# Hymba layer on one core: the first output projection's scalings spread over its last norm steps, five of eight transposes within the last query product

## The chip, the core and the metric

One core of a Trainium2 chip. The metric is the device time of one execution in microseconds, as a median over runs. The engines are TensorE (PE in the profile, its weight loads PEld), VectorE (DVE), ScalarE (ACT), GpSimd (POOL) and the DMA queues, which are issued by SyncE (SP) and POOL.

## What is computed

One decoder layer, cut to what matters here; rmsnorm divides a row by its root mean square and multiplies it by a gain.

```python
def layer(x, attend, ..., w_in, w_out, w_up, w_down):
    proj = rmsnorm(x, g_mix_pre) @ w_in
    q, k, v, xl, gate = jnp.split(proj, ...)
    attn = attend(q, k, v)              # stick-breaking attention
    lru = rglru_branch(xl, ...)         # recurrent branch
    mixed = jnp.concatenate([attn, lru * gelu(gate)], axis=-1) @ w_out
    x = x + rmsnorm(mixed, g_mix_post)
    u = jax.nn.relu(rmsnorm(x, g_mlp_pre) @ w_up)
    x = x + rmsnorm((u * u) @ w_down, g_mlp_post)
```

The prompt has 2048 rows and 16 meta tokens, the model 1024 columns, the MLP 4096; 64 sample rows run along. All is float32.

## The kernel before

**Products.** Every float32 operand is split into a high part and a residue (ahi and alo, whi and wlo, uh and ul), and a product is three matmuls per chunk of 128 of the 1024 inner columns: high x high, residue x high, high x residue. In `gemm` they are L184 to L186, with 8 chunks k to one output tile of 128x512; `work.tick` at L190 stands behind chunks 2, 5 and 7. In `gemm_nat` (L194) they are L216 to L218; it serves the output and the down projections. Weights come by DMA into wraw (two buffers); ACT copies them to whi (L161), DVE subtracts to get wlo (L162), two buffers each, one tile ahead.

**Blocks.** The 2048 prompt rows are four blocks s of 512. `inproj` (L434) runs for each s: recurrent branch, keys, values, then `queries` (L588), a generator that yields after each of four query products. At the last block the generator is held back: its products c = 0 and 1 run ahead of the first block's output projection, c = 2 and 3 (the last) behind it.

**Attention** runs on the side. `attn` is a generator of small steps, each with up to three things: logits (L706, into T), then sigmoids, a scan (L650), a carry copy (L653) and a product (L654) on ACT and DVE; the transposing of finished weights beta (L716, into T), which ACT and DVE split into wth (L727) and wtl (L728); and the product with the values (L738, L740, into O). `Work` deals the steps out: `tick(c)` earns c times a rate of engine time and takes steps until it is spent, `burst(us)` takes steps worth that many microseconds at once, `need` takes steps until the named block's attention is finished. PE runs in the order in which the program is written; the order of the other engines' instructions is set by the framework's scheduler.

**The first output projection.** `Group.out_proj` (L987) multiplies the mixed rows of the first block by w_out, in four row blocks j, whose results are y0 to y3 (128x1024 each). `follow(n)` does the norms behind it: `added` (L1003) adds x to the normed y, stores x1 (L1005) and lets ACT sum its squares; `rstd_of` (L236 or L238 on DVE, L240 on POOL) makes the factor by a power. Two `follow` calls and four scalings `normed(j)` (L1010) are left to the caller as a list `todo`: entries 0 and 1 are `follow(3)` and `follow(4)`, entries 2 to 5 scale y0 to y3. `xpose(k)` transposes column block k of all four y (L264, four 128x128 transposes into T); ACT scales that into ahi (L266) and DVE makes alo (L267), both in the tiles that the up products read. Eight such groups come ahead of the first up product.

Ahead of the change the order is: output projection, `todo[0]`, query product 2, `todo[1]`, query product 3, the four scalings, a burst of 4.0, and eight times `xpose(k)` with a burst of 0.5. Then up (`up`, eight products of 128x512) and down (`down`) alternate, four times for each block. The other blocks' output projections stand before the last down products of the block ahead, with a `need` for their attention in front (`group`, L1172), and their norms within those down products.

Of the kernel before, what the change touches and what calls it, by code (L numbers as in the profile page):

```python
# [18 lines left out]
KC = 8  # L19
# [63 lines left out]
def program(tc, I, O, NSB, NSC):  # L83
    with tc.manual_schedule(engines={ET.PE}):
        _program(tc, I, O, NSB, NSC)


def _program(tc, I, O, NSB, NSC):
# [3 lines left out]
    work = Work()  # L92
# [24 lines left out]
    def psD():  # L117
        return T(ps, [P, 512], F32, "D", 4)

    def psT():  # L120
        return T(ps, [P, 512], F32, "T", 3)
# [43 lines left out]
    def w_next():  # L165
        n = wpos[0]
        wpos[0] += 1
        w_split(n)
        w_load(n + 1)
        w_split(n + 1)  # L170
        w_load(n + 2)
        return wsp.pop(n)

    def gemm(ahi, alo, chunks, after_k=None, before_k=None):

        whi, wlo = (t.rearrange("p (k m) -> p k m", k=KC) for t in w_next())
        outs = []
        for ci, (a, b) in enumerate(chunks):
            acc = psD()
            o = acc[:, 0:b - a]  # L180
            for k in range(KC):
                if before_k is not None:
                    before_k(ci, k)
                nc.tensor.matmul(o, whi[:, k, :], ahi(k, a, b), start=(k == 0), stop=False)  # L184
                nc.tensor.matmul(o, whi[:, k, :], alo(k, a, b), start=False, stop=False)  # L185
                nc.tensor.matmul(o, wlo[:, k, :], ahi(k, a, b), start=False, stop=(k == KC - 1))  # L186
                if after_k is not None and ci == len(chunks) - 1:
                    after_k(k)
                if k in (2, 5, 7):
                    work.tick(0.64 * (b - a) / SB * (3 if k < 7 else 2))  # L190
            outs.append(o)
        return outs
# [67 lines left out]
    def xpose_k(ys, k, gT, hi, lo):  # L260

        t = psT()
        for j, y in enumerate(ys):
            nc.tensor.transpose(t[:, j * P:(j + 1) * P], y[:, k * P:(k + 1) * P], ident)  # L264
        n = len(ys) * P
        nc.scalar.activation(hi[:, 0:n], t[:, 0:n], AF.Identity, scale=gT[:, k:k + 1])  # L266
        nc.vector.scalar_tensor_tensor(lo[:, 0:n], t[:, 0:n], gT[:, k:k + 1], hi[:, 0:n].bitcast(F32),  # L267
                                       op0=ALU.mult, op1=ALU.subtract)
# [154 lines left out]
    def prep(s):  # L423

        ys = []
        for j in range(4):
            y = T(xp_, [P, DM], F32, "y", 4)
            nc.sync.dma_start(y, xsrc(s, j))
            r = rstd_of([mean_sq(y, P)], P)
            nc.vector.tensor_scalar(y, y, r, None, op0=ALU.mult)  # L430
            ys.append(y)
        return ys

    def inproj(s, p1, pa, K, ahi, alo, before_k=None):  # L434
# [8 lines left out]
        def stage(nm, d, bufs=2):  # L443
            return T(p1 if nm == "sf" else pa, [P, W], d, nm, bufs)
# [143 lines left out]
        def queries():  # L588
            ys = None
            for c in range(4):  # L590
                nxt = None
                if c == 2 and s + 1 < NSB:
                    ys = prep(s + 1)
                if c == 3 and s + 1 < NSB:
                    def nxt(k):
                        if k > 0:
                            xpose_k(ys, k - 1, K["g_pre"], ahi[:, k - 1], alo[:, k - 1])
                outs = gemm(hi_, lo_, chunks, after_k=nxt)
                if nxt is not None:
                    nxt(KC)  # L600
                hi, lo = stage("sh", F32R), stage("sl", F32R)
                for (a, b), o in zip(chunks, outs):
                    nc.scalar.copy(hi[:, a:b], o)
                    nc.vector.tensor_tensor(lo[:, a:b], o, hi[:, a:b].bitcast(F32), op=ALU.subtract)
                for e, t in ((0, hi), (1, lo)):
                    nc.sync.dma_start(qd[s][2 * c:2 * c + 2, :, e, :].rearrange("h p n -> (h p) n"), t[:, o0:o0 + SB].bitcast(F32))
                if s == 0:
                    a0 = NP - chunks[1][0]
                    for hh in range(2):
                        src = outs[1][64 * hh:64 * hh + 64, a0:a0 + NSAMP].rearrange("p (t b q) -> p t b q", t=4, b=2)  # L610
                        for bb in range(2):
                            e0 = 16 * bb + 8 * hh
                            nc.scalar.copy(K["Qz"][64 * hh:64 * hh + 64, c, :, bb, e0:e0 + 8], src[:, :, bb, :])
                yield
            work.ready.add(("kv", s))

        return queries()

    def lru_outputs(s, K):
# [539 lines left out]
    for s in range(NSB):  # L1159
        work.rate = RATE0 if s else 0.0  # L1160
        queries = inproj(s, p1, pa, K, ahi, alo, first if s == 0 else None)
# [5 lines left out]
    def gain(p, n):  # L1167
        t = T(p, [P, DM], F32, n)
        nc.sync.dma_start(t, I[n].unsqueeze(0).to_broadcast([P, DM]))
        return t  # L1170

    def group(s):  # L1172
        if s == NSB - 1:
            for i in range(NSB):
                work.need(("a", i))
            close(att, "right")
            px = pool("last", side="right")
            hi = T(px, [P, KC, SB + 2 * NSAMP], F32R, "ahi3")
            lo = T(px, [P, KC, SB + NSAMP], F32R, "alo3")
        else:  # L1180
            work.need(("a", s))
            px, hi, lo = None, act2[0], act2[1]
        return Group(s, hi, lo, px, pacc, K, gB)


    next(queries)
    work.need("s")
# [4 lines left out]
    cur = group(0)  # L1192
# [5 lines left out]
    for _ in ld:  # L1198
        pass
    cur.out_proj()  # L1200
    cur.todo[0]()
    next(queries, None)
    cur.todo[1]()
    next(queries, None)
    for f in cur.todo[2:]:
        f()
    for _ in queries:
        pass
    close(pa, "right")
    work.rate = RATE2  # L1210
    pmlp = pool("pmlp")
    gB.append(gain(pmlp, "g_mlp_post"))
    work.burst(BURST)
    for k in range(KC):
        cur.xpose(k)
        work.burst(0.5)
    pu, later = None, None
    for s in range(NSB):
        nxt = None
# [4 lines left out]
        for sc in range(NSC):  # L1224
# [3 lines left out]
            if end and s + 1 < NSB:  # L1228
                nxt = group(s + 1)
# [23 lines left out]
        cur = nxt  # L1253
# [4 lines left out]

NQ = 2
LATER = 2  # L1260
RATE0, RATE1, RATE2, RATE3, RATE4, BURST = 0.2, 0.5, 0.5, 0.55, 0.3, 4.0


def layout(inputs, NSB=4, NSC=4):
# [78 lines left out]
```

## Time and profile before

| what | value |
|---|---|
| median of 3 runs | 2711.2 us (2709.44 to 2712.72) |
| the profiled execution, its own time | 2709.24 us |
| its span, first to last instruction | 2707.4 us |
| mean granted clock of TensorE | 0.995 |
| busy: PE, DVE, ACT, POOL | 2657.4, 1836.6, 1451.9, 358.6 us |

The clock is a share of full speed. Busy time of PE is modelled at its ends: matmuls overlap, so the distance between starts is what one costs in a dense stretch. Timelines give a start in us from the span's begin, a duration, and in brackets the idle time before with what ended it.

### The profile page before, as it was taken

How to read it: one execution, taken by the hardware profiler on the slowest of the kernel's cores; microseconds unless marked ns; L12 is line 12 of the kernel's file. 1: busy time of each engine (PE TensorE's matmuls, PEld its weight loads, DVE VectorE, ACT ScalarE, POOL GpSimd, SP SyncE). 2: the span in 40 equal slices, each digit the busy share in tenths (PEclk: the TensorE clock that was granted, in tenths of full speed). 3: DMA queues.
4: the chain of work that ended last, by engine and by line, in shares of the span. 5: the costliest groups of instructions: out<-in, count | busy, mean ns of one | idle time of the engine just before them, and what ended most of it. 6: DMA issues, size and time to landing. Idle time of an engine off the chain costs nothing.

```text
span 2707.4 us, 36910 instructions
## 1 busy us (share of the span) xinstructions
PE 2657.4 (98%) x13804; PEld 2201.8 (81%) x13804; DVE 1836.6 (68%) x2898; ACT 1451.9 (54%) x2430; POOL 358.6 (13%) x579
## 2 busy tenths in 40 slices
PE   8999999999899999999999999999999999999997
PEld 7987778778788888878888888878888888898895
DVE  6555477876877777869677777796787747343344
ACT  6566476865656554546565555665555535332232
POOL 3122331111211101011100110110000001000002
PEclk9999999999999999999999999999999999999999
DMA  5466867485444433455433334543333244222223
GB/s 174 138 216 199 270 178 221 127 232 182 136 130 121 115 110 105 135 165 158 112 105 120 102 112 127 156 151 111 103 107 97 84 156 162 85 84 81 81 84 108
DMA packets 149156, 368.12 MB, mean 136 GB/s; under 512 B 20992, under 2 KB 51200, under 8 KB 148976
## 3 DMA queue, kind: packets, MB, share of 16 engines
q1 hardware_dynamic: 103792, 287.35, 32.8%
q0 software_dynamic: 45184, 78.41, 11.7%
q8 instruction: 109, 1.79, 0.3%
q14 instruction: 71, 0.58, 0.1%
HBM read 305.51 MB, written 60.04 MB: 135 GB/s over the span
## 4 chain that ended last, share of the span: by engine, by line
PE 88%; DVE 4%; issue 3%; POOL 1%; ACT 1%; DMA 1%; SPq 0%; POOLq 0%; DVEq 0%; ACTq 0%
PE D L184 12%; PE D L186 12%; PE D L185 12%; PE D L216 11%; PE D L217 11%; PE D L218 11%; PE T L716 5%; PE T L706 4%; PE O L738 2%; PE O L740 2%; PE D L455 1%; POOL kv L843 1%; PE O L222 1%; PE O L221 1%; PE T L264 1%
## 5 line engine op out<-in xcount | busy, mean ns | idle before, releaser
L162 DVE TENSOR_TENSOR wlo<-wraw,whi 128x1024 fp32r<-128x1024 f32 x368 | 453.5, 1232 | 448.8 <-ACT whi L161 445.5
L184 PE MATMUL D<-ahi,whi 128*128 128x512 f32 (+3 forms) x1920 | 705.2, 367 | 0.0
L186 PE MATMUL D<-ahi,wlo 128*128 128x512 f32 (+3 forms) x1920 | 682.1, 355 | 0.3 <-DVE carry L653 0.3
L185 PE MATMUL D<-alo,whi 128*128 128x512 f32 (+3 forms) x1920 | 680.5, 354 | 1.7 <-DVE alo L410 1.3
L161 ACT CAST whi<-wraw 128x1024 fp32r<-128x1024 f32 x368 | 386.7, 1051 | 487.8 <-PE D L217 301.1
L216 PE MATMUL D<-whi,uh 128*128 128x512 f32 x1024 | 417.0, 407 | 1.9 <-DVE ms L236 1.9
L217 PE MATMUL D<-whi,ul 128*128 128x512 f32 x1024 | 404.4, 395 | 0.0
L218 PE MATMUL D<-wlo,uh 128*128 128x512 f32 x1024 | 403.9, 394 | 0.0
L184 PEld LDWEIGHTS D<-ahi,whi 128*128 128x128 f32 x1920 | 361.9, 189 | 50.2 <-issue 7.1
L186 PEld LDWEIGHTS D<-ahi,wlo 128*128 128x128 f32 x1920 | 361.4, 188 | 50.1 <-DVE wlo L162 0.7
L185 PEld LDWEIGHTS D<-alo,whi 128*128 128x128 f32 x1920 | 362.3, 189 | 43.0 <-issue 1.7
L642 ACT ACTIVATE keep<-T,nbias 128x512 f32<-128x512 f32 (+6 forms) x352 | 210.0, 596 | 230.2 <-PE T L706 225.1
L650 DVE TENSOR_TENSOR_SCAN pb<-keep,carry 128x513 f32<-128x513 f32 (+1 forms) x228 | 267.9, 1175 | 57.1 <-ACT keep L642 54.8
L728 DVE TENSOR_TENSOR wtl<-T,wth 128x512 fp32r<-128x512 f32 (+1 forms) x320 | 191.0, 602 | 86.6 <-ACT wth L727 85.7
L727 ACT CAST wth<-T 128x512 fp32r<-128x512 f32 (+1 forms) x320 | 166.6, 523 | 142.6 <-PE T L716 141.5
L218 PEld LDWEIGHTS D<-wlo,uh 128*128 128x128 f32 x1024 | 192.2, 188 | 46.6
L216 PEld LDWEIGHTS D<-whi,uh 128*128 128x128 f32 x1024 | 192.5, 188 | 41.7 <-DVE ms L236 2.3
L217 PEld LDWEIGHTS D<-whi,ul 128*128 128x128 f32 x1024 | 192.9, 188 | 38.6
L643 ACT ACTIVATE beta<-T,bias 128x512 f32<-128x512 f32 (+6 forms) x352 | 208.3, 592 | 0.0
L654 DVE TENSOR_TENSOR beta<-beta,pb 128x512 f32<-128x512 f32 (+7 forms) x360 | 203.2, 564 | 0.0
L716 PE MATMUL T<-ident,beta 128*128 128x128 f32 (+1 forms) x1216 | 192.3, 275 | 2.9 <-ACT beta L643 2.5
L706 PE MATMUL T<-kv,q 128*128 128x512 f32 (+5 forms) x640 | 177.6, 359 | 2.1 <-DVE alo L267 1.7
(235 smaller groups left out, 3472.1 us busy)
## 6 DMA issues: line engine op xcount, KB each, us to landing
wraw<-in_w_up SPq DMA_DIRECT2D x128, 512.0 KB, 3.5
wraw<-in_w_down SPq DMA_DIRECT2D x128, 512.0 KB, 3.5
wraw<-in_w_in SPq DMA_DIRECT2D x64, 512.0 KB, 4.0
q<-qd POOLq DMA_DIRECT2D x64, 256.0 KB, 4.3
wraw<-in_w_out SPq DMA_DIRECT2D x32, 512.0 KB, 3.8
kv<-kd POOLq DMA_DIRECT2D x48, 256.0 KB, 3.2
kv<-vd POOLq DMA_DIRECT2D x48, 256.0 KB, 3.8
y<-in_x_prompt SPq DMA_DIRECT2D x16, 512.0 KB, 6.9
```

Of the source, the lines that this page charges most:

```text
L161: nc.scalar.copy(hi, r)
L162: nc.vector.tensor_tensor(lo, r, hi.bitcast(F32), op=ALU.subtract)
L184: nc.tensor.matmul(o, whi[:, k, :], ahi(k, a, b), start=(k == 0), stop=False)
L185: nc.tensor.matmul(o, whi[:, k, :], alo(k, a, b), start=False, stop=False)
L186: nc.tensor.matmul(o, wlo[:, k, :], ahi(k, a, b), start=False, stop=(k == KC - 1))
L216: nc.tensor.matmul(o, h, whi[:, kk, :], start=st, stop=False)
L217: nc.tensor.matmul(o, l, whi[:, kk, :], start=False, stop=False)
L218: nc.tensor.matmul(o, h, wlo[:, kk, :], start=False, stop=sp)
L642: nc.scalar.activation(keep[:, o:512], S, AF.Sigmoid, bias=nbias, scale=-0.125)
L650: nc.vector.tensor_tensor_scan(pb[:, o:513][:, ::-1], kr, kr, 1.0 if carry is None else carry, op0=ALU.mult, op1=ALU.bypass)
L706: nc.tensor.matmul(o, H["q"][:, e, i * P:(i + 1) * P], kap, start=(e == 0), stop=(e == 1))
L716: nc.tensor.transpose(t[0:kn, i * P:(i + 1) * P], w[:, c0:c0 + kn], ident)
```

## The change

The two `follow` calls and the four scalings are dealt out anew: `follow(3)` and the scalings of y0 and y1 before query product 2, `follow(4)` and the scaling of y2 behind it, that of y3 within query product 3, behind chunk k = 1. Within the same product the transposes of column blocks 0 to 4 stand behind chunks 3 to 7. Column blocks 5 to 7 follow it with a burst of 0.5 each. The burst of 4.0 and five bursts of 0.5 are gone.

```diff
--- before.py
+++ after.py
@@ -595,8 +595,10 @@
                     def nxt(k):
                         if k > 0:
                             xpose_k(ys, k - 1, K["g_pre"], ahi[:, k - 1], alo[:, k - 1])
+                if c == 3 and s + 1 == NSB:
+                    nxt = between
                 outs = gemm(hi_, lo_, chunks, after_k=nxt)
-                if nxt is not None:
+                if nxt is not None and s + 1 < NSB:
                     nxt(KC)
                 hi, lo = stage("sh", F32R), stage("sl", F32R)
                 for (a, b), o in zip(chunks, outs):
@@ -1182,6 +1184,13 @@
             px, hi, lo = None, act2[0], act2[1]
         return Group(s, hi, lo, px, pacc, K, gB)
 
+    def between(k):
+
+        if k == 1:
+            todo[5]()
+        if k >= 3:
+            cur.xpose(k - 3)
+
 
     next(queries)
     work.need("s")
@@ -1198,20 +1207,19 @@
     for _ in ld:
         pass
     cur.out_proj()
-    cur.todo[0]()
-    next(queries, None)
-    cur.todo[1]()
-    next(queries, None)
-    for f in cur.todo[2:]:
+    todo = cur.todo
+    for f in (todo[0], todo[2], todo[3]):
         f()
+    next(queries)
+    todo[1]()
+    todo[4]()
     for _ in queries:
         pass
     close(pa, "right")
     work.rate = RATE2
     pmlp = pool("pmlp")
     gB.append(gain(pmlp, "g_mlp_post"))
-    work.burst(BURST)
-    for k in range(KC):
+    for k in range(KC - 3, KC):
         cur.xpose(k)
         work.burst(0.5)
     pu, later = None, None
@@ -1258,7 +1266,7 @@
 
 NQ = 2
 LATER = 2
-RATE0, RATE1, RATE2, RATE3, RATE4, BURST = 0.2, 0.5, 0.5, 0.55, 0.3, 4.0
+RATE0, RATE1, RATE2, RATE3, RATE4 = 0.2, 0.5, 0.5, 0.55, 0.3
 
 
 def layout(inputs, NSB=4, NSC=4):
```

The order on DVE, from the residue of query product 3's weights on (wlo_6748 before, wlo_6750 now; y_6377, y_6388, y_6420 and y_6442 are y0 to y3; pb and beta are attention, sl is query product 2's residue). Before:

```order
L162 TENSOR_TENSOR wlo_6748<-wraw_6632,whi_6747 128x1024
L653 COPY carry_6731<-pb_6727 128x1
L654 TENSOR_TENSOR beta_6726<-beta_6726,pb_6727 128x512
L236 TENSOR_SCALAR ms_6743<-ss_6737 128x1
L1003 SCALAR_TENSOR_TENSOR y_6442<-y_6442,rstd_6741,x_6707 128x1024
L162 TENSOR_TENSOR wlo_6813<-wraw_6751,whi_6812 128x1024
L749 TENSOR_TENSOR pb_6779<-O_6393,pb_6779 64x512
L650 SCALAR_TENSOR_TENSOR pb_6790<-keep_293_1884,carry_6567 128x401
L604 TENSOR_TENSOR sl_6798<-D_6753,sh_6797 128x512
L653 COPY carry_6794<-pb_6790 128x1
L654 TENSOR_TENSOR beta_6789<-beta_6789,pb_6790 128x400
L236 TENSOR_SCALAR ms_6808<-ss_6806 128x1
```

Now:

```order
L162 TENSOR_TENSOR wlo_6750<-wraw_6632,whi_6749 128x1024
L1012 TENSOR_SCALAR y_6388<-y_6388,rstd_6719 128x1024
L1005 SCALAR_TENSOR_TENSOR y_6442<-y_6442,rstd_6741,x_6707 128x1024
L751 TENSOR_TENSOR pb_6781<-O_6393,pb_6781 64x512
L652 SCALAR_TENSOR_TENSOR pb_6792<-keep_293_1884,carry_6567 128x401
L606 TENSOR_TENSOR sl_6800<-D_6755,sh_6799 128x512
L655 COPY carry_6796<-pb_6792 128x1
L656 TENSOR_TENSOR beta_6791<-beta_6791,pb_6792 128x400
L236 TENSOR_SCALAR ms_6810<-ss_6808 128x1
L1012 TENSOR_SCALAR y_6420<-y_6420,rstd_6745 128x1024
L162 TENSOR_TENSOR wlo_6816<-wraw_6753,whi_6815 128x1024
L1012 TENSOR_SCALAR y_6442<-y_6442,rstd_6812 128x1024
```

Before, the four scalings came behind these rows; now y0's stands four rows ahead of the first, and y1's, y2's and y3's among them, while the residue of the first up weights (wlo_6813, now wlo_6816) went from behind y3's addition to behind y2's scaling.

The order on PE within query product 3 (D is its accumulator, T_6837 a logit tile), around its fourth and fifth chunk now. Before, from chunk 4 on:

```order
L184 MATMUL D_6818<-ahi_101,whi_6747 128x512
L185 MATMUL D_6818<-alo_102,whi_6747 128x512
L186 MATMUL D_6818<-ahi_101,wlo_6748 128x512
L184 MATMUL D_6818<-ahi_101,whi_6747 128x512
L185 MATMUL D_6818<-alo_102,whi_6747 128x512
L186 MATMUL D_6818<-ahi_101,wlo_6748 128x512
L706 MATMUL T_6837<-kv_6509,q_6396 128x400 x2
L184 MATMUL D_6818<-ahi_101,whi_6747 128x512
L185 MATMUL D_6818<-alo_102,whi_6747 128x512
L186 MATMUL D_6818<-ahi_101,wlo_6748 128x512
L184 MATMUL D_6818<-ahi_101,whi_6747 128x512
L185 MATMUL D_6818<-alo_102,whi_6747 128x512
```

Now, from chunk 2 on:

```order
L184 MATMUL D_6821<-ahi_101,whi_6749 128x512
L185 MATMUL D_6821<-alo_102,whi_6749 128x512
L186 MATMUL D_6821<-ahi_101,wlo_6750 128x512
L184 MATMUL D_6821<-ahi_101,whi_6749 128x512
L185 MATMUL D_6821<-alo_102,whi_6749 128x512
L186 MATMUL D_6821<-ahi_101,wlo_6750 128x512
L264 MATMUL T_6835<-ident_72,y_6377 128x128
L264 MATMUL T_6835<-ident_72,y_6388 128x128
L264 MATMUL T_6835<-ident_72,y_6420 128x128
L264 MATMUL T_6835<-ident_72,y_6442 128x128
L184 MATMUL D_6821<-ahi_101,whi_6749 128x512
L185 MATMUL D_6821<-alo_102,whi_6749 128x512
```

The first group of y transposes stands behind chunk 3, and four more groups follow in the same way, one behind each chunk.

The order on PE where attention ends (T are beta transposes, O products with values, D the gemm). Before, within an up product of the third block:

```order
L184 MATMUL D_21200<-ahi_1191_6136,whi_21121 128x512
L185 MATMUL D_21200<-alo_1192_6137,whi_21121 128x512
L186 MATMUL D_21200<-ahi_1191_6136,wlo_21122 128x512
L738 MATMUL O_20684<-wth_21164,kv_20762 128x512
L740 MATMUL O_20684<-wtl_21165,kv_20762 128x512
L738 MATMUL O_20684<-wth_21181,kv_20762 128x512
L184 MATMUL D_21200<-ahi_1191_6136,whi_21121 128x512
L185 MATMUL D_21200<-alo_1192_6137,whi_21121 128x512
L186 MATMUL D_21200<-ahi_1191_6136,wlo_21122 128x512
```

Now, ahead of the third block's last down products:

```order
L742 MATMUL O_20819<-wtl_21232,kv_20901 128x512
L718 MATMUL T_21259<-ident_72,beta_21062 16x128
L718 MATMUL T_21259<-ident_72,beta_21096 16x128
L718 MATMUL T_21259<-ident_72,beta_21116 16x128
L718 MATMUL T_21259<-ident_72,beta_21165 16x128
L740 MATMUL O_20819<-wth_21242,kv_20901 128x512
L742 MATMUL O_20819<-wtl_21243,kv_20901 128x512
L740 MATMUL O_20819<-wth_21253,kv_20901 128x512
L742 MATMUL O_20819<-wtl_21254,kv_20901 128x512
L740 MATMUL O_20819<-wth_21264,kv_20901 128x512
L216 MATMUL D_21283<-whi_21146,uh_20715 128x512
L217 MATMUL D_21283<-whi_21146,ul_20716 128x512
```

The last attention rows stood between up products; now six groups of beta transposes and fifteen products stand together, behind the last up product and ahead of the first down product.

## Rows read from the trace of the kernel before

**Rows 1.** The page's busy table: us, share of the span, instructions.

```profile
PE 2657.4 (98%) x13804; PEld 2201.8 (81%) x13804; DVE 1836.6 (68%) x2898; ACT 1451.9 (54%) x2430; POOL 358.6 (13%) x579
```

**Rows 2.** Busy times by stretches: stretch, its length, busy us (instructions) of each engine, clock, DMA.

```profile
680.00:700.00 20.00, 14.07 (x77) 10.73 (x76) 19.04 (x39) 13.35 (x27) 8.60 (x10) 0.83 0.81 218
```

**Rows 3.** PE timeline, last query to first up product: start, duration, [idle <-releaser].

```profile
674.98 0.50 PE L186 MATMUL D<-ahi,wlo 128*128 128x512 f32 x1 [0.26 <-DVE carry L653]
...
680.56 0.53 PE L706 MATMUL T<-kv,q 128*128 128x400 f32 x2
...
683.15 0.55 PE L716 MATMUL T<-ident,beta 128*128 128x128 f32 x3 [1.26 <-ACT beta L643]
...
704.87 0.63 PE L706 MATMUL T<-kv,q 128*128 128x400 f32 x2 [0.90 <-DVE alo L267]
...
705.34 0.40 PE L184 MATMUL D<-ahi,whi 128*128 128x512 f32 x1
```

**Rows 4.** Busy times in steps of 2 us, after the last query product.

```profile
686.00:688.00 2.00, 0.95 (x3) 0.75 (x3) 2.00 (x5) 0.00 (x0) 0.07 (x1) 0.50 0.96 221
...
690.00:692.00 2.00, 2.00 (x11) 2.00 (x10) 1.85 (x3) 1.15 (x2) 0.00 (x0) 0.50 0.79 127
...
692.00:694.00 2.00, 1.68 (x15) 1.44 (x13) 1.55 (x3) 1.55 (x4) 0.55 (x1) 0.93 0.88 258
```

**Rows 5.** Timeline of PE within the output projection's second half.

```profile
655.03 0.39 PE L738 MATMUL O<-wth,kv 128*128 128x512 f32 x1
...
655.50 0.51 PE L706 MATMUL T<-kv,q 128*128 128x384 f32 x2
...
655.84 0.60 PE L716 MATMUL T<-ident,beta 128*16 128x128 f32 x4
...
656.20 0.48 PE L216 MATMUL D<-whi,ahi 128*128 128x512 f32 x1
```

**Rows 6.** Timeline of DVE around the last two query products.

```profile
673.70 1.22 DVE L162 TENSOR_TENSOR wlo<-wraw,whi 128x1024 fp32r<-128x1024 f32 x1
...
675.57 1.28 DVE L1003 SCALAR_TENSOR_TENSOR y<-y,rstd,x 128x1024 f32<-128x1024 f32 x1
...
676.76 1.22 DVE L162 TENSOR_TENSOR wlo<-wraw,whi 128x1024 fp32r<-128x1024 f32 x1
...
680.58 0.14 DVE L236 TENSOR_SCALAR ms<-ss 128x1 f32<-128x1 f32 x1
...
684.71 0.74 DVE L1010 TENSOR_SCALAR y<-y,rstd 128x1024 f32<-128x1024 f32 x1
```

**Rows 7.** Groups by form from 674 to 706: count, busy us, mean ns, idle before.

```profile
L266 ACT ACTIVATE ahi<-T,gT 128x512 fp32r<-128x512 f32 x8 | 5.5, 690 | 1.0 <-PE T L264 1.0
...
L267 DVE SCALAR_TENSOR_TENSOR alo<-T,gT,ahi 128x512 fp32r<-128x512 f32 x7 | 5.1, 724 | 0.5 <-ACT ahi L266 0.5
...
L650 DVE TENSOR_TENSOR_SCAN pb<-keep,carry 128x401 f32<-128x401 f32 x4 | 4.2, 1042 | 0.0
...
L728 DVE TENSOR_TENSOR wtl<-T,wth 128x512 fp32r<-128x512 f32 x5 | 3.4, 682 | 0.3 <-ACT wth L727 0.3
...
L654 DVE TENSOR_TENSOR beta<-beta,pb 128x400 f32<-128x400 f32 x4 | 2.2, 561 | 0.0
```

**Rows 8.** Line L1005 (stores of x1): from issue to landing.

```profile
DMA to landing us min/median/max: 2.6/4.9/7.0
```

**Rows 9.** Timeline of POOL: the powers behind two of the statistics.

```profile
663.64 0.57 POOL L240 TENSOR_TENSOR rstd<-ms,nhalf 128x1 f32<-128x1 f32 x1 [13.43 <-DVE ms L238]
...
680.87 3.75 POOL L240 TENSOR_TENSOR rstd<-ms,nhalf 128x1 f32<-128x1 f32 x1 [1.40 <-DVE ms L236]
```

**Rows 10.** Timeline of PE: the last attention product, the next down product.

```profile
2164.66 0.39 PE L738 MATMUL O<-wth,kv 128*128 128x512 f32 x1
...
2173.83 0.39 PE L216 MATMUL D<-whi,uh 128*128 128x512 f32 x1
```

**Rows 11.** Busy times in 2 us, last output projection, around its longest pause.

```profile
2252.00:2254.00 2.00, 0.85 (x4) 0.72 (x5) 2.00 (x6) 1.85 (x5) 0.77 (x2) 1.00 0.80 324
```

## The prediction

> **What bounds the kernel now.** The page's busy table comes first: TensorE (PE) 2657.4 us of a span of 2707.4, 98% [rows 1]. PE issues in program order, so a saving must come from places where it waits or runs slow. The busy times by stretches show one such place within the change: from 680 to 700 us PE is busy 14.07 of 20 us at a granted clock of 0.83 [rows 2]. PE's timeline shows what stands there. The last query product ends at 680.56, then come the burst of attention steps and the eight groups of transposes, and the first up product starts at 705.34 [rows 3]: 24.8 us. PE waits there for attention operands and, near the end, for residues: 1.26 us at 683.15, 0.90 us at 704.87 [rows 3]. The clock is at its lower level (0.50) in 686 to 688 and 690 to 692, after the first of those waits, and at 0.93 in 692 to 694 [rows 4].
>
> What should these 24.8 us cost PE? From the distances between starts in a gemm: two 128x512 products in 0.47 us, so 0.23 each; a 384-column logit pair 0.34; four transposes 0.36 [rows 5]. The burst's last part and the transposes hold 8 groups of y transposes (2.9), three short groups of beta transposes and two 400-column logits (1.6), and the attention that the change moves out, 7.6 (below). That is 12.1, so **12.7 us are waiting and half rate**. VectorE (DVE) is the engine without gaps there: it does residues of 0.72 us, scans of 1.04, products of 0.56 and weight residues of 1.2 in one queue [rows 6, 7].
>
> **The change, part by part.**
>
> *Scalings earlier.* Scaling y0 and y1 now stands ahead of the residue of the last query product's weights. That residue ran at 673.70 for 1.22 us, and PE's first product with it already waited 0.26 us, until 674.98 [rows 3, 6]. Now one scaling (0.74 by the row at 684.71) and the carry copy, product and statistic that ran behind it (675.57 - 673.70 - 1.2 = 0.7) come first: it ends at 673.7 + 0.7 + 0.7 + 1.2 = 676.3. PE waits 1.4 us more. Behind the wait stand all products of the last query.
>
> *Transposes within the query.* A step is three products, 0.70 us. Four steps from 676.3 bring PE's queue to the first transposes at 678.8. They need y3, the last block. Its chain: the addition ran at 675.57 [rows 6] and now stands behind two scalings but ahead of the weight residue of 676.76, so it starts at 675.57 + 2 x 0.7 = 677.0 and ends at 678.2. The statistic ran at 680.58 [rows 6]; behind the same attention and query rows it moves by two scalings less one residue, to 680.8. Then POOL's power, then the scaling of y3. DVE meanwhile does y2 (0.7) and the first up weights' residue (1.2), to 682.7. The scaling also waits until the store of y3, issued at 678.2, has landed, 4.9 us later by the median [rows 8]: 683.1. So y3 is ready at about 683.9, and **PE waits 5.1 us** in the middle of the query, with the rest of it queued behind. The bounds: by the shortest store (2.6) and power (0.57, row at 663.64) DVE's own queue sets 683.4; by the longest store (7.0) it is 678.2 + 7.0 + 0.7 = 685.9. I take the median, the row of the same store.
>
> That price is the open one: 0.57 us at 663.64, 3.75 at 680.87 while DVE scaled [rows 9]. The Trainium skill, GPSIMD Engine Reference, section 1 Specifications, says that GpSimd shares its SBUF interfaces with VectorE and contends with instructions that use both read ports or read two SBUF tensors. Both kinds are queued behind the statistic here; by that rule the power is held until DVE falls idle at 682.7 and ends by 683.3, y3 is ready at 684.0, and the sum is 0.1 us larger. Taken from the rows alone, the short one ends before the store has landed and changes nothing; the long one ends at 684.6, and the sum is 1.5 us larger. I leave the sum at the store's landing.
>
> *What follows the wait.* Before, the clock was low from about 686 to 692, after waits that began at 682 [rows 3, 4]. I expect the same here from about 683 to 689: a step and a group of transposes then cost 1.4 + 0.7 = 2.1 us. The first residue starts at 683.9 + 0.2 (its last transpose) + 0.7 (ScalarE's copy [rows 7]) = 684.9, the third at 689.1. From there DVE has no gap: until the seventh residue it does five residues (5 x 0.66), two scans with carry and product (2 x 1.5), one weight residue (1.15), the query's residue and one attention residue (0.6 each, all as distances between starts): 8.7 us, to 697.8. The last transposes wait for that residue, and the first up product starts at 698.2. That is **7.1 us earlier** than 705.34. At full clock the third residue would start at 687.0: 696.1.
>
> *What is moved out.* The order shows which rows left the stretch: eleven 512-column attention products (11 x 0.23 = 2.6), two each of 384, 256 and 128 columns (0.7 by columns), 21 beta transposes (1.9), logits of 128, 256, 384, 512, 512 and 400 columns (2.0 by columns) and some five returns to gemm operands at 0.09: 7.6 us of PE time. They are done later, in gemms where PE is the bound, so this is paid again in full. The place as a whole: 705.3 - 698.2 - 7.6 = **0.5 us lost**. With the bounds above it gains 1.6 (full clock) or loses 2.5 (late store).
>
> *The end of attention.* Before, attention ran out at 2164.66, 9 us ahead of the down product at 2173.83 [rows 10]. Everything being eleven steps late, the last ones now stand bare between the last up product and that down product: six groups of transposes (2.1) and fifteen products (3.5), 5.6 us of PE time, counted above as moved. What is new is waiting. DVE must do five residues (0.6 each), one of 16 rows with its memset (1.2), a weight residue (1.15) and the last up tile's two rows (1.2), 6.6 us, starting about 1 us after PE, because that weight's copy needs PE's last product. So PE is through after 7.6 to 7.7 us: **2.1 us of waiting**. From below, 1 us (only the last pieces wait); from above, 5.6 more if all of it runs at half rate. I take 2.1: such short waits left the clock at 1.00 in 2252 to 2254, where PE was busy 0.85 of 2 us [rows 11]. The loads of the last group's attention output follow 1.5 us behind, and their use is 22 us of down products away; they cost nothing unless that cover goes.
>
> *At nothing:* the instructions themselves, whose number is unchanged; DMA issues on SP and POOL, which change places with weights loaded two tiles ahead.
>
> **Sum.** 0.5 + 2.1 = 2.6 us slower: 2709.24 becomes 2711.8 in the profiled execution, which stands 2.0 below the median of the three runs (2711.2); the median becomes **2713.8 us**. A measurement of this kernel tells about 0.2%, 5.4 us, from no change, so this is no difference that could be told.
>
> **Rivals.**
>
> *The bare end runs at half rate (slower).* Place: the bare steps before the last group's down products. If PE pauses there as much as it did from 682 to 688, the clock falls, and some 6 us at half rate cost 3.0 more: 0.5 + 2.1 + 3.0 = 5.6, 2716.8 us. It decides once DVE begins that stretch 2 us late, which doubles the waiting. For it: DVE's queue is the longer one there. Against: [rows 11]. With the late store as well, 2718.8.
>
> *The clock survives the query (a little faster).* The wait is split: y0, y1 and y2 are transposed before y3 is there, at 678.8 and 681.6. If that keeps the clock, the place gains 1.6; if the end also waits only 1 us, 2710.6 us. Against: the fall in [rows 4] came after waits as broken.
>
> *The transposes do not wait (faster).* If y3 is ready when PE arrives, most of the 12.7 us goes. It would need the statistic and store 5 us earlier than the rows say. DVE's queue then starts near 680, and the up product near 692: 13.3 earlier, less 7.6 and 2.1: 3.6 us faster, 2707.6; with a hidden end 2705.5.
>
> **How the numbers follow.** Chances: the forecast 0.50 (own range 2710.6 to 2715.8, by the bounds of the place and of the end), half rate at the end 0.22, clock survives 0.16, no wait 0.12. The range reaches to the no-wait case below and the late-store end above: 2707.0 to 2719.5. Faster by over 0.2% is the better part of the no-wait case and what I may have misread: 0.12; slower by over 0.2% is the half-rate case: 0.22; the rest, 0.66, lies within.
>
> **What would show it.** Right: in the last query PE waits some 1.8 us at its first low-weight product and some 5 us at the first y transposes, in pieces that end with the scalings; the clock is near 0.5 for 6 us after; the first up product starts 7 us earlier than before; and at the last group's end, 2 us of PE waits for attention residues without gemm products between. Wrong: no wait at the y transposes, the first up product before 694 or after 702, or a granted clock under 0.9 at the bare end.

## The result, and the profile after

The changed kernel takes 2716.0 us by its median, the kernel before, in the same comparison, 2711.9. The ratio is 1.0015, 95% interval 1.0008 to 1.0021: 4.1 us slower, between 2.2 and 5.7. The forecast was 2.6 us slower, within 0.2%, and so it is. The interval leaves out 1, so with 15 executions of each kernel the slowing can be told, which the prediction thought it could not. But the parts of the sum came out otherwise than forecast, and two experiments (e2 and e3) say the opposite of one of its steps. The profiled execution has a span of 2714.2 us, 6.8 above the one before.

The busy table of the changed kernel answers to [rows 1]: 5.6 us more of busy PE with the same instructions, which goes with the stretches of low clock below.

```profile
PE 2663.0 (98%) x13804; PEld 2206.7 (81%) x13804; DVE 1837.1 (68%) x2898; ACT 1450.4 (53%) x2430; POOL 350.2 (13%) x579
```

PE's timeline of the changed kernel, from the last query product to the first up product (columns as in [rows 3]):

```profile
676.59 0.50 PE L186 MATMUL D<-ahi,wlo 128*128 128x512 f32 x1 [1.53 <-DVE wlo L162]
...
679.01 0.38 PE L264 MATMUL T<-ident,y 128*128 128x128 f32 x2
681.85 0.33 PE L264 MATMUL T<-ident,y 128*128 128x128 f32 x1 [2.46 <-DVE y L1012]
684.53 0.47 PE L264 MATMUL T<-ident,y 128*128 128x128 f32 x1 [2.35 <-DVE y L1012]
...
693.13 0.63 PE L708 MATMUL T<-kv,q 128*128 128x400 f32 x2 [0.70 <-DVE alo L267]
694.92 0.66 PE L718 MATMUL T<-ident,beta 128*128 128x128 f32 x4 [1.16 <-DVE alo L267]
...
699.58 0.78 PE L184 MATMUL D<-ahi,whi 128*128 128x512 f32 x1
```

The waits that were forecast are there: 1.53 us at the first product with the low weights, then two transposes (y0 and y1), 2.46 us for y2, 2.35 for y3. DVE's timeline of the changed kernel shows the cause of each:

```profile
673.93 0.74 DVE L1012 TENSOR_SCALAR y<-y,rstd 128x1024 f32<-128x1024 f32 x1
...
675.32 1.21 DVE L162 TENSOR_TENSOR wlo<-wraw,whi 128x1024 fp32r<-128x1024 f32 x1
...
681.72 1.21 DVE L162 TENSOR_TENSOR wlo<-wraw,whi 128x1024 fp32r<-128x1024 f32 x1
683.72 0.75 DVE L1012 TENSOR_SCALAR y<-y,rstd 128x1024 f32<-128x1024 f32 x1 [0.79 <-DMA x1d<-y]
```

y0's scaling stands ahead of the weight residue; y3's waits at the end for the store of x1 (the DMA in brackets). Busy times in 2 us show what was not forecast (columns as in [rows 2]):

```profile
684.00:686.00 2.00, 1.47 (x4) 1.17 (x5) 0.71 (x2) 0.69 (x1) 0.00 (x0) 0.50 0.87 253
...
690.00:692.00 2.00, 2.00 (x15) 1.70 (x14) 1.94 (x4) 2.00 (x4) 0.00 (x0) 1.00 0.00 0
...
696.00:698.00 2.00, 1.33 (x5) 0.78 (x5) 2.00 (x5) 1.54 (x4) 0.48 (x1) 0.54 1.04 356
698.00:700.00 2.00, 2.00 (x10) 1.83 (x10) 2.00 (x4) 1.27 (x3) 0.60 (x2) 0.50 0.80 219
700.00:702.00 2.00, 2.00 (x6) 1.52 (x6) 1.81 (x5) 0.49 (x2) 0.00 (x0) 0.50 1.09 242
702.00:704.00 2.00, 2.00 (x9) 1.59 (x8) 0.00 (x0) 0.00 (x0) 0.00 (x0) 0.76 0.30 61
```

The clock is low twice: after the waits for y, as forecast, and again from 696 to 703, through the last transposes and half of the first up product. Before, [rows 4] shows one such stretch.

The end of attention, PE's timeline of the changed kernel, answers to [rows 10]:

```profile
2169.98 0.39 PE L186 MATMUL D<-ahi,wlo 128*128 128x512 f32 x1
...
2173.15 0.50 PE L742 MATMUL O<-wtl,kv 128*128 128x512 f32 x1 [0.30 <-DVE wtl L730]
...
2178.72 0.47 PE L740 MATMUL O<-wth,kv 128*128 128x512 f32 x1 [1.49 <-DVE wth L726]
2179.03 0.39 PE L216 MATMUL D<-whi,uh 128*128 128x512 f32 x1
```

Waits of 1.49 + 0.30 = 1.8 us, at a clock of 1.00. From the last up product's last matmul to the down product it is 9.05 us; before, it was 0.23, as the same two rows of the kernel before say:

```profile
2173.60 0.40 PE L186 MATMUL D<-ahi,wlo 128*128 128x512 f32 x1
2173.83 0.39 PE L216 MATMUL D<-whi,uh 128*128 128x512 f32 x1
```

For one ledger of the 6.8 us, one window serves for both kernels and for all experiments: from the first matmul of the third query product to the first of the second up product, called **the place** below. Before:

```profile
667.92:712.34 44.42, 37.14 (x184) 29.23 (x182) 42.10 (x78) 32.63 (x59) 18.42 (x20) 0.92 0.66 195
```

After:

```profile
668.25:709.36 41.11, 32.24 (x144) 25.55 (x143) 29.38 (x51) 22.02 (x39) 10.20 (x11) 0.83 0.57 180
```

The start of the place is 0.3 later (668.25 - 667.92); the place itself 3.3 shorter (44.42 - 41.11), though it holds 40 rows of PE less; from there to the last up product 0.6 shorter; the end of attention 8.8 longer (9.05 - 0.23); the rest 1.6 longer (2714.2 - 2179.03 against 2707.4 - 2173.83). That is 6.8. The 1.6 is a low clock in the last output projection of the changed kernel, after a pause of 1.90 us that both kernels have ([rows 11]; at 2258 after):

```profile
2256.00:2258.00 2.00, 0.45 (x2) 0.01 (x1) 1.60 (x2) 1.88 (x5) 0.36 (x1) 1.00 0.60 244
2258.00:2260.00 2.00, 1.66 (x6) 1.38 (x7) 2.00 (x5) 1.10 (x2) 1.58 (x2) 0.86 0.70 281
2260.00:2262.00 2.00, 2.00 (x6) 1.54 (x6) 1.62 (x5) 0.00 (x0) 1.06 (x2) 0.50 0.36 53
```

Of the fourteen profiles in this study seven show that low clock after that pause and seven don't, whether attention ends bare or not. From the row behind that pause to the end of the span it is 455.8 to 455.9 us in the seven with it and 454.3 in the seven without. So it is left out of what is blamed on the change: without it the profiled executions differ by 5.2 us, the medians by 4.1.

### The profile page after: what moved, and what is told of

It reads as the page before. It is cut to its first block, busy times and chain, and to the rows that moved or that the text cites. A ratio compares the mean times of both kernels' runs of the same rounds, so it can differ in the third digit from the quotient of the medians.

```text
span 2714.2 us, 36903 instructions
## 1 busy us (share of the span) xinstructions
PE 2663.0 (98%) x13804; PEld 2206.7 (81%) x13804; DVE 1837.1 (68%) x2898; ACT 1450.4 (53%) x2430; POOL 350.2 (13%) x579
## 4 chain that ended last, share of the span: by engine, by line
PE 91%; DVE 4%; DMA 1%; ACT 1%; issue 1%; POOL 1%; SPq 0%; DVEq 0%; POOLq 0%; ACTq 0%
PE D L184 13%; PE D L186 13%; PE D L185 13%; PE D L216 11%; PE D L217 11%; PE D L218 11%; PE T L718 5%; PE T L708 4%; PE O L740 2%; PE O L742 2%; PE D L455 1%; DVE wlo L162 1%; PE T L264 1%; PE O L222 1%; PE O L221 1%
```

## The experiments

All ratios are to the kernel before in the same comparison (its median there was 2711.9 us for the change and 2710.4 to 2710.7 for the experiments), with 95% intervals; place, PE's idle time (length less busy) and mean clock come from the window above, found in each profile by the same two matmuls.

| run | median us | ratio | place us | idle | clock |
|---|---|---|---|---|---|
| before | 2711.9 | | 44.42 | 7.3 | 0.92 |
| the change | 2716.0 | 1.0015 [1.0008, 1.0021] | 41.11 | 8.9 | 0.83 |
| e1 change, RATE2 0.52 | 2716.8 | 1.0020 [1.0011, 1.0029] | 40.67 | 8.9 | 0.83 |
| e2 before without bursts | 2709.0 | 0.9993 [0.9984, 1.0002] | 35.05 | 5.6 | 0.95 |
| e3 change with burst | 2717.2 | 1.0018 [1.0009, 1.0028] | 49.08 | 11.4 | 0.86 |
| e4 scalings alone | 2712.3 | 1.0005 [0.9994, 1.0016] | 46.53 | 8.2 | 0.89 |
| e5 scalings, no bursts | 2710.6 | 1.0001 [0.9992, 1.0010] | 37.73 | 6.4 | 0.86 |
| e6 three groups within | 2714.1 | 1.0014 [1.0005, 1.0023] | 38.86 | 9.7 | 0.91 |
| e7 e2, three queries behind | 2716.0 | 1.0020 [1.0011, 1.0029] | 39.81 | 4.3 | 0.96 |
| e8 change, three behind | 2718.0 | 1.0029 [1.0013, 1.0044] | 41.01 | 3.7 | 0.92 |
| e9 e2, first block 0.545 | 2716.8 | 1.0019 [1.0009, 1.0029] | 36.16 | 5.8 | 0.95 |
| e10 change, first block 0.545 | 2721.7 | 1.0036 [1.0023, 1.0049] | 42.06 | 9.1 | 0.84 |
| e11 e9, scalings on ScalarE | 2714.8 | 1.0016 [1.0006, 1.0025] | 34.61 | 5.0 | 0.95 |
| e12 change, scalings on ScalarE | 2712.8 | 1.0005 [0.9996, 1.0013] | 37.57 | 7.6 | 0.91 |

The place holds 144 matmul rows in the change, e2, e5 and e6 and 145 in e12, so these five lengths can be set against each other. e7 and e8 have one more query product in it and 172 rows each, e9, e10 and e11 eight rows more of attention, e3 and e4 the bursts. Up to the first up product the rows are the same, form by form, in the change, e2, e5, e6 and e9 to e12. Single profiles repeat there: the change, e1 and e10, alike up to that point, need 31.33, 31.17 and 31.44 us, e2 and e9 26.85 and 26.86.

### Which part costs: e1 to e4

e1, against the change:

```diff
-RATE0, RATE1, RATE2, RATE3, RATE4 = 0.2, 0.5, 0.5, 0.55, 0.3
+RATE0, RATE1, RATE2, RATE3, RATE4 = 0.2, 0.5, 0.52, 0.55, 0.3
```

> The changed kernel with RATE2 0.52 in place of 0.50: attention finishes within the third block's up products again, so that no attention steps stand bare ahead of the last down products; the place of the change stays as it is. My theory (the bare end costs its waits, 1.5 + 0.3 us by the trace of the changed kernel, and nothing else): 1.8 us less than the changed kernel, about 2.4 us above the kernel before (ratio 1.0009), no PE wait for L726 or L730 there, the attention products being hidden in gemms that PE bounds. Rival (the low clock at 2259 to 2263 comes from that end as well): 3.5 us less, ratio 1.0003. Rival (the waits only move): ratio still 1.0015.

The waits at the end of attention went, and the time did not fall: 1.0020. The rival that the waits only move fits; where to is shown with e9.

e2, against the kernel before:

```diff
-    work.burst(BURST)
     for k in range(KC):
         cur.xpose(k)
-        work.burst(0.5)
+        if k >= 5:
+            work.burst(0.5)
```

> The kernel before, in which only the burst of 4.0 and five of the eight bursts of 0.5 are gone: scalings and transposes stay behind the last query product. My theory (what costs is that 7.6 us of attention leave a place that DVE bounds and are paid for later, plus the bare end's 1.8): the first up product about 6 us earlier than before, 7.6 of PE work later and 1.8 of waits, in sum 2 to 4 us above the kernel before (ratio 1.0007 to 1.0015), nearly what the whole change costs. Rival (the loss is made by the scalings and transposes that PE waits for within the query): no loss, ratio 1.0000 or below.

My theory fell here. The same eleven steps leave the place, the same bare end follows, with 1.48 and 0.30 us of waits, and the kernel is no slower than before. The window of e2:

```profile
667.74:702.79 35.05, 29.48 (x144) 23.00 (x143) 29.48 (x51) 22.26 (x39) 13.55 (x11) 0.95 0.64 211
```

The place is 9.4 us shorter than before, which pays for the 8.8 at the end. With the same 144 rows the changed kernel needs 41.11 - 35.05 = 6.1 us more: that is the price of moving scalings and transposes. Of it 3.3 us are idle time (8.9 against 5.6): 1.4 more at the weight residue, 1.0 more at the y transposes (4.8 against 3.8, since e2 waits for y as well, behind the query), 1.0 more at later operands. The rest is low clock.

e3, against the change:

```diff
+    work.burst(6.5)
     for k in range(KC - 3, KC):
```

> The changed kernel with the lost attention given back: a burst of 6.5 behind the last query product, ahead of the last three groups of transposes. My theory: the place grows by what DVE needs for these steps, some 7 to 8 us, so that the first up product stands at about 707; the bare end's 1.8 us and the 7.6 us paid later are saved: 0 to 3 us above the kernel before (ratio 1.0000 to 1.0011). Rival (waits and low clock within the query are the whole loss): ratio 1.0015 as for the change.

The first up product stood at 706.7, as expected, and the bare end was gone, but the ratio is 1.0018, as the rival had it; its interval reaches down to 1.0009, into the range of my theory. The place is 4.7 us longer than before (49.08 against 44.42) with most of its rows given back (173 of 184): the loss is there.

e4, against the change:

```diff
-        if k >= 3:
-            cur.xpose(k - 3)
...
-    for k in range(KC - 3, KC):
+    work.burst(4.0)
+    for k in range(KC):
         cur.xpose(k)
```

> The scalings dealt out as in the change, but all eight groups of transposes behind the last query product with all bursts (4.0, then eight of 0.5), as in the kernel before. My theory: PE waits 1.5 us at the first low-weight product of the query instead of 0.26, the query ends some 1.3 us later, and behind it DVE has three or four scalings less to do (2 to 3 us): within 1.5 us of the kernel before on either side, ratio 0.9995 to 1.0005. Rival (the early scalings are what costs): 2 us or more above, ratio over 1.0007.

The ratio, 1.0005, is within what was expected, but its interval does not part the two theories. The place is 2.1 us longer than before (46.53 against 44.42) for the same rows, at a lower clock (0.89 against 0.92).

### Scalings or transposes: e5 and e6

e5, against the change:

```diff
-        if k >= 3:
-            cur.xpose(k - 3)
...
-    for k in range(KC - 3, KC):
+    for k in range(KC):
         cur.xpose(k)
-        work.burst(0.5)
+        if k >= 5:
+            work.burst(0.5)
```

e6 has the same three bursts and, against the change:

```diff
-        if k >= 3:
-            cur.xpose(k - 3)
+        if k >= 5:
+            cur.xpose(k - 5)
...
-    for k in range(KC - 3, KC):
+    for k in range(3, KC):
```

> The changed kernel with all eight groups of transposes behind the last query product and nothing else changed (no burst of 4.0, three of 0.5). It differs from the changed kernel by the place of five groups alone, and from the run without bursts by the scalings alone. Theory 1 (the transposes within the query make the loss: PE meets y3's chain with the rest of the query queued behind it, twice at half rate): waits and half rate from the output projection to the end of the first up product 7 to 8.5 us instead of 14.4, one stretch of low clock, ratio 0.9995 to 1.0005. Theory 2 (the early scalings do it, as in the run of the scalings alone, 12.1 against 9.6): 9.5 to 10.5 us there, ratio 1.0004 to 1.0012.

> The changed kernel with three groups of transposes within the last query product instead of five, behind chunks 5, 6 and 7, the other five behind it. Theory 1a (the loss grows with the part of the query that is held behind y3): the first transposes come 1.4 us later, so that PE waits about 3.4 us for y2 and y3 instead of 4.8; two steps instead of four run after it; second stretch of low clock gone: 10 to 11 us of waits and half rate, ratio 1.0003 to 1.0010. Theory 1b (any transposes within the query cost the same): 14 us, ratio 1.0015.

The window of e5:

```profile
666.74:704.47 37.73, 31.30 (x144) 25.29 (x143) 29.37 (x51) 22.41 (x39) 10.20 (x11) 0.86 0.62 197
```

So at equal work the place grows from 35.05 (e2) to 37.73 by the early scalings, 2.7 us, and from there to 41.11 by the five groups within the query, 3.4 us. The ratios go the same way, 0.9993, 1.0001, 1.0015. The intervals of the first two overlap; those of e5 and of the change touch only at their ends. Both theories were half right. Of the 2.7 us 1.0 and of the 3.4 us 0.6 are in the first up product, at a low clock. That e5 would have one stretch of low clock was wrong: it is at 0.50 from 684 to 690, and again at 0.52 in 694 to 696. e6 waits 4.7 us for y, as the change does, not 3.4 as expected, has one stretch of low clock, and a place 1.1 us above e5; its ratio, 1.0014, is higher than that explains. In the profiled executions 2.2 of the 3.5 us between e6 and e5 (spans 2713.2 and 2709.7) stand ahead of the place, which starts at 668.95 against 666.74, before any row that was moved; for the medians it stays open.

Does the wait for y come with the transposes? PE's timeline of e5 says that it is there without them too, but shorter, since the query's four steps are done meanwhile:

```profile
675.08 0.50 PE L186 MATMUL D<-ahi,wlo 128*128 128x512 f32 x1 [1.53 <-DVE wlo L162]
...
683.56 1.98 PE L264 MATMUL T<-ident,y 128*128 128x128 f32 x9 [2.42 <-DVE y L1012]
```

### DVE's queue: e12 and e11

e12, against the change; e11 has the same edit in e9:

```diff
-                nc.vector.tensor_scalar(self.ys[j][:rows], x1s_[j][:rows], r2[j][:rows], None, op0=ALU.mult)
+                if self.s == 0:
+                    nc.scalar.activation(self.ys[j][:rows], x1s_[j][:rows], AF.Identity, scale=r2[j][:rows])
+                else:
+                    nc.vector.tensor_scalar(self.ys[j][:rows], x1s_[j][:rows], r2[j][:rows], None, op0=ALU.mult)
```

> The changed kernel with the first block's four scalings on ScalarE: the residue of the last query's weights no longer stands behind y0's scaling on DVE. If that wait and DVE's queue are the loss: PE waits 0.3 us there instead of 1.5, y2 and y3 are scaled at most 1 us earlier, place 11 to 13 us instead of 14.4, ratio 1.0006 to 1.0012. If the loss is that transposes stand in front of the query's steps before y3's chain can end: place 13 to 15 us, two stretches of low clock, ratio 1.0012 to 1.0020.

PE's timeline of e12:

```profile
680.98 0.48 PE L264 MATMUL T<-ident,y 128*128 128x128 f32 x1 [3.59 <-ACT y L1013]
682.40 0.48 PE L264 MATMUL T<-ident,y 128*128 128x128 f32 x1 [0.94 <-ACT y L1013]
```

PE no longer waits for the weight residue (1.53 us in the change). For y it still waits 4.5 us (3.59 + 0.94), against 4.8, now for ScalarE's scalings, but the last y is met 14.8 us after the start of the place instead of 16.3 (682.40 - 667.62 against 684.53 - 668.25). The place is 37.57 instead of 41.11, and the second stretch of low clock is gone: the clock is 1.00 in 692 to 698. The ratio is 1.0005, no measurable difference from before, but its interval also overlaps that of the change. So the edit takes 3.5 us off the place; how much of that is loss of the change needs e11. The Trainium skill, Perfetto Trace Analysis, section Optimizing Scalar/DVE Operations, says that work which either engine can do may be given to ScalarE when DVE is saturated; this trace agrees: DVE is busy 2.00 of every 2 us from 676 to 682 in the change, and the place is 3.5 us shorter.

> The first of these runs, with the first block's four scalings on ScalarE instead of DVE. If DVE's queue is what the transposes wait for: it has 2.8 us less to do between 680 and 686, the last scaling and the first residue stand 1 to 2 us earlier, place 5 to 6 us: ratio 0.9976 to 0.9986. If the chain of y3 (statistic, power, store) or ScalarE's own queue is: no difference from that run beyond 0.0004.

The place is 1.55 us shorter than in e9, in the direction of the first case, though the ratio (1.0016 against 1.0019) can't show it. So 1.55 of the 3.5 us would be gained without the change as well. With the scalings on ScalarE the moves still cost 4.1 us up to the first up product, for the same rows (e11, then e12):

```profile
668.43:693.73 25.30, 20.26 (x99) 15.79 (x98) 22.70 (x39) 22.74 (x37) 10.37 (x11) 0.93 0.84 275
```

```profile
667.62:696.99 29.37, 21.82 (x100) 16.62 (x98) 22.38 (x39) 23.76 (x38) 10.36 (x11) 0.88 0.66 227
```

With the scalings on DVE they cost 4.5 there (31.33 against 26.85 in e2). What DVE's queue adds to the loss of the change is thus about 2 us, 1.6 of them the second stretch of low clock in the first up product; the other 4.1 stay where PE meets the transposes within the query.

### More PE work over y3's chain: e7 and e8

e7, against e2 (e8 does the same to the change: `follow(3)` stands ahead of the added product, `follow(4)` and the scalings of y0 and y1 behind it):

```diff
     cur.todo[1]()
     next(queries, None)
+    next(queries, None)
...
-NQ = 2
+NQ = 1
```

> The kernel before with three query products behind the output projection instead of two (NQ 1) and without the burst of 4.0 and five bursts of 0.5: transposes and scalings behind the query. If the waits at the place are those of y3's chain (5.6 us of PE work more now lie beside it): waits and half rate there 2 to 4 us instead of 7.2, so 3 to 5 us below the run without bursts, ratio 0.9975 to 0.9985. If DVE's queue is the bound there (the residues of the third query product and its weights come into it as well): no gain, ratio 0.9990 to 1.0000.

> The changed kernel with three query products behind the output projection instead of two (NQ 1): the second and third follow-up of the norms one product later each than the scalings allow, y3's scaling and five groups of transposes within the last product as in the change. If what costs is that PE reaches the transposes before y3 is scaled: no wait of PE for y there, at most one stretch of low clock, waits and half rate 4 to 7 us instead of 14.4, ratio 0.9980 to 0.9992. If it is the transposes' own work on ScalarE and DVE within the query: still over 10 us, ratio over 1.0003.

In the place PE's idle time falls, to 4.3 and 3.7 us with one more product in it, but both kernels are slower. The loss is 60 us earlier: the query product taken away had covered the loads of the first block's mixed rows. PE's timeline of e8, and below it that of ACT, which waits for the first load (PE waits 4.37 us there in e7, and not at all in the kernel before and in the change):

```profile
609.93 0.79 PE L216 MATMUL D<-whi,ahi 128*128 128x512 f32 x1 [4.25 <-ACT ahi L968]
...
608.83 1.04 ACT L968 CAST ahi<-x 128x1024 fp32r<-128x1024 f32 x1 [2.36 <-DMA x<-md]
```

So both forecasts of the ratio failed. But in the place e8 did what its first case said. PE does not wait for y within the last query product:

```profile
680.49 0.60 PE L264 MATMUL T<-ident,y 128*128 128x128 f32 x4
```

There is one stretch of low clock, from 692 to 699, and for the same rows the place is only 1.2 us longer than in e7 (e7, then e8):

```profile
666.34:706.15 39.81, 35.56 (x172) 28.31 (x170) 35.65 (x61) 25.17 (x46) 8.56 (x11) 0.96 0.64 213
```

```profile
663.82:704.83 41.01, 37.29 (x172) 28.76 (x170) 35.21 (x61) 25.20 (x46) 9.69 (x11) 0.92 0.63 206
```

Up to the first up product e8 is even 0.7 us shorter (31.23 against 31.96); the rest is that low clock. So the same moves cost 6.1 us where PE meets the transposes before y3 is scaled, and 1.2 where it meets them after. The wait for the weight residue is 0.4 us in e7 and in e8.

### Making the attention up elsewhere: e9 and e10

Against e2 and against the change:

```diff
-            work.rate = RATE2
+            work.rate = RATE2 + (0.045 if self.s == 0 else 0.0)
```

> The run without bursts, and in the up products of the first block a rate of 0.545 in place of 0.5, so that the eleven steps are made up there and attention ends within the third block's up products as in the kernel before. If the bare end costs its waits and the rest of the program keeps its order: 1.8 us below the run without bursts, ratio 0.9984 to 0.9990 to the kernel before, waits and half rate at the place 7 us, none at the end. If waits only move (as with the raised rate in all blocks, where the third output projection waited more): ratio 0.9992 to 1.0002.

> The changed kernel with the same rate of 0.545 in the first block's up products alone: no bare end, and the other blocks' output projections meet the attention that they met before. My theory (the place costs some 4 us, the bare end 1.8): ratio 1.0006 to 1.0012, place 14 us of waits and half rate, end none. Rival (a raised rate costs as much as it saves, as in the run of all blocks): 1.0015 to 1.0022.

Both expectations failed: e9 is 1.0019 where e2 is 0.9993, e10 1.0036. DVE's timeline of e9, in the up products that follow the third output projection, beside the norms that end the block ahead:

```profile
1786.46 1.27 DVE L1130 SCALAR_TENSOR_TENSOR acc<-acc,rstd,g_mlp_post 128x1024 f32<-128x1024 f32 x1
1787.66 0.67 DVE L1072 TENSOR_TENSOR ul<-uf,uh 128x512 fp32r<-128x512 f32 x1
1788.26 1.21 DVE L1131 TENSOR_TENSOR x<-acc,x 128x1024 f32<-128x1024 f32 x1
1789.40 1.21 DVE L162 TENSOR_TENSOR wlo<-wraw,whi 128x1024 fp32r<-128x1024 f32 x1
```

and PE's, of the same kernel:

```profile
1790.66 0.67 PE L186 MATMUL D<-ahi,wlo 128*128 128x512 f32 x1 [3.58 <-DVE wlo L162]
```

In the kernel before the same residue ran ahead of these two rows:

```profile
1784.76 1.21 DVE L162 TENSOR_TENSOR wlo<-wraw,whi 128x1024 fp32r<-128x1024 f32 x1
1786.41 1.29 DVE L1130 SCALAR_TENSOR_TENSOR acc<-acc,rstd,g_mlp_post 128x1024 f32<-128x1024 f32 x1 [0.45 <-POOL rstd L240]
```

With attention a few steps further on, the scheduler put the weight residue behind a norm, and PE waited 3.58 us, more than the waits of the bare end (1.8). e10 shows the same wait (3.58), e1 one of 2.18. The clock was 0.50 in 1792 to 1794 behind that wait, and again after the pause in the last output projection. The wait is half of the 7.1 us between the spans of e9 (2714.2) and e2 (2707.1), and the low clock after that last pause 1.5; the rest is not told apart term by term.

## Why the prediction was right, and where its steps failed

- *Place and time of the waits*: right. The low-weight product was forecast at 676.3 and stood at 676.59; the wait for y 5.1 us from 678.8, measured 2.46 + 2.35 from 679.0, split as the second rival had it; y3 forecast at 683.9, ready at 684.5 (683.72 + 0.75). The store of x1 did gate it. POOL's power, the open price, took 2.07 us here, from 681.28, and ended at 683.35, 0.4 after DVE fell idle (681.72 + 1.21 = 682.9). That is as the prediction worked out from the rule that GpSimd shares its SBUF interfaces with VectorE and contends with some of its instructions (the Trainium skill, GPSIMD Engine Reference, section 1 Specifications). It is one case, and the store hid it.
- *The low clock*: the step "from about 683 to 689 ... From there DVE has no gap ... At full clock" failed. The first stretch came as forecast, with residues 2.1 us apart (685.76, 687.90, 690.03). The second, 696 to 703, was in no case. It costs 1.6 us in the first up product alone (9.78 us there; e2 and e12 do the same rows at full clock in 8.20), and the first up product starts at 699.58, not 698.2. (The first residue's sum, 683.9 + 0.2 + 0.7, is 684.8, not 684.9; that changes nothing.)
- *The place as a whole*: forecast 7.1 us earlier, measured 6.1 to the first up product (37.42 us against 31.33) and 1.6 given back in it, so 4.5. That is the term that was mis-sized, by 2.6 us: 7.6 - 4.5 = 3.1 lost, where 0.5 was forecast and 2.5 was its bound.
- *The moved attention and its end*: forecast 7.6 of PE work and 2.1 of waits, 9.7; measured 8.8 there, with waits of 1.8. The price held, and the clock stayed at 1.00 from 2170 to 2180, so the first rival fell.
- *What the sum hid*: the forecast put the loss on the moved attention and on the bare end. e2 has both and is not slower, since taking the bursts away shortens the place by 9.4 us. The change gains that and loses 6.1 of it by its own moves, 2.7 by the scalings and 3.4 by the transposes within the query. e8 adds that moves of this kind cost 1.2 us where y3 is ready in time, so most of the 6.1 comes from PE meeting the transposes before that. The forecast of the sum was right because it compared with the kernel before, not because its reason was; and that it came so near is partly luck, since its place was 2.6 us too fast and its price of the moved attention 0.9 too high.
- *Still open*: why the second stretch of low clock comes. Waits of 0.48, 1.16 and 0.91 us from 690 to 696 in e12 left the clock at 1.00; waits of 1.41 and 0.29 us in e5 did not. It came in every profile with five groups within the query and the scalings on DVE (the change, e1, e3, e10, and e8, where it is the only one), also in e5, and in none of e2, e4, e6, e9, e11 and e12.

No version here is shown to be faster than the kernel before: e2, at 0.9993, reaches to 1.0002.

## What to carry to other kernels

Where one engine issues in program order, work that needs a late operand is not brought forward by putting it between products that don't: the rest of the product is then queued behind the operand. Before moving a helper's step ahead, read what stands next in that helper's queue; the same step on another engine may give back part of what the move lost (here ScalarE, 3.5 us at the place, 1.55 of which it gave without the move as well). Side work that is moved shifts everything after it, so look at the schedule of the far stages too: eleven steps more or less changed a wait by 3.6 us a thousand microseconds later.

## What the runs showed of the hardware

The same pause of 1.9 us in the last output projection was followed by a clock of 1.00 throughout in seven profiles and by a stretch at 0.50, worth 1.6 us, in seven others, with the same wait for the same statistic ahead of it. Each profile is of another kernel, so that one kernel does both is not shown by them. But no edit stands in that projection, and the low clock came with a bare end and without, so a difference of that size between two profiles should not be put down to an edit. The mean granted clock of the kernel before lay between 0.992 and 0.995 over its 29 executions in the last comparison.
